# Low parts of weight blocks by a negation on GpSimd and an adding DMA, in a two-layer diffusion backbone

## The chip, the cores and the metric

The kernel runs on one core of one Trainium2 chip, in one launch. The metric is the device time of that launch in microseconds. Engines are named as in the profile: PE is TensorE (matmuls), DVE is VectorE, ACT is ScalarE, POOL is GpSimd, SP is SyncE, which issues nearly all DMAs here.

## The reference

Two layers of a backbone over 256 latent tokens and 256 context tokens, model width 1024, float32 throughout. Each layer is a half-step SwiGLU FFN, a mixing step and a second half-step FFN, each with adaLN shift, scale and gate computed from a condition vector.

```python
def ffn_sublayer(x, m, i, g, w_in, w_out):
    u = modulate(rms_norm(x, g), m, i)
    return x + 0.5 * m[:, 3 * i + 2][:, None] * swiglu(u, w_in, w_out)

# mixing, per layer
p = u @ w_in                    # q, k, v, Fourier input, gate logits
a = (rms_norm(attn_heads, subln_g) * (1 - lam_init)) @ w_attn_out
fr = fourier_mix(f) @ w_four_out
merged = sigmoid(ga + b_gate[0]) * a + sigmoid(gf + b_gate[1]) * fr
x = x + gate * (merged @ w_o)
```

Attention is differential (two softmax maps per head). The context stream is needed only until layer 1 has its keys and values: from there on, the merge, the output projection and the last FFN work on the latent tokens alone. A final RMSNorm gives the output.

## The kernel before

Activations stand transposed: features on the 128 partitions, tokens along the free dimension, 512 columns for both streams (latent and context) and 256 for the latent one alone. Every float32 product is made of three fast matmuls. A number is split into a high part, rounded to the matmul's format (`F32R`), and a low part, the rest; `mm3` (L370 to L375) accumulates high x high, high x low and low x high. `mm_wide` (L377 to L381) does the same for 256 columns with two matmuls, the first one over both parts of the activations at once.

The weights, 392 blocks of 128 x 1024 float32 (512 KB each, eight 128 x 128 tiles), pass through the class `Stream`. Its steps for a block:

- `load_to` (L176): SP issues the DMA of the raw block into a slot, `wraw`.
- `split_pieces` (L192, L193): ACT copies `wraw` to `whi`, which rounds it; then DVE or POOL computes `wlo = wraw - whi`.
- `next` hands out block b. It first issues loads up to b + `ahead[0]` and splits up to b + `ahead[1]`. `ahead` is (6, 2) while both streams are computed, (7, 4) in the last FFN and (7, 3) in the merge of layer 1.

The string `lo_on` says who subtracts: its letter at position i modulo its length stands for block i, "v" for DVE, "p" for POOL. All instructions run in the order in which the code issues them on each engine (`manual_schedule`); waits between engines follow from the tiles. `wraw`, `whi`, `wlo`, the activations `u` and `g` and more share one pool of 46 slots of 4 KB per partition, so a load also waits until the slot it takes over is free.

In an FFN the loop over j (L663 on) takes two blocks per step, one for `pa` and one for `pb`; ACT and DVE then make `silu(pa) * pb` (`silu`, `gv`) and split it into `g`. `project_out` multiplies `g` or the merged branches by the output weights (`po`). In layer 0, `tick` adds to every block two dot products on DVE (`junk`, L302) of condition weights (`mraw`, loaded by SP, 512 KB each) and every other time a small POOL instruction `mval` (L315, L317); these make the adaLN values. POOL also adds up squares for the norms (`acc`, L424).

The stages whose splits the change touches are the FFNs, the merge with its gates (`pg`, `pao`, `pfo`) and the output projection; the heads' projections, the values and the very first blocks keep DVE and POOL as before.

Of the kernel before, what the change touches and what calls it, by code (L numbers as in the profile page):

```python
# [11 lines left out]
F32 = mybir.dt.float32  # L12
F32R = mybir.dt.float32r
BF16 = mybir.dt.bfloat16
AF = mybir.ActivationFunctionType
ALU = mybir.AluOpType
# [21 lines left out]
LAT, CTX = 0, 1  # L38
# [33 lines left out]

BEGUN = 3

E_AHEAD, E_LO, E_K = 4, "vp", 2

SQ_PARTS = [7, 5]

# [80 lines left out]
    return rope.reshape(P, 4 * S), np.ascontiguousarray(dft.astype(np.float32))  # L159


class Stream:


# [15 lines left out]
    def split_pieces(self, n):  # L180

        nc = self.nc
        i = self.n_split
        self.n_split += 1
        raw = self.raw.pop(i)
        hi = self.pool.tile([P, 1024], F32R, tag="s", name="whi")
        lo = self.pool.tile([P, 1024], F32R, tag="s", name="wlo")
        self.hl[i] = (hi, lo)
        eng = nc.gpsimd if self.lo_on[i % len(self.lo_on)] == "p" else nc.vector
        for j in range(n):  # L190
            c = slice(j * (1024 // n), (j + 1) * (1024 // n))
            nc.scalar.activation(hi[:, c], raw[:, c], AF.Copy)  # L192
            eng.tensor_tensor(out=lo[:, c], in0=raw[:, c], in1=hi[:, c].bitcast(F32), op=ALU.subtract)  # L193
            yield
# [25 lines left out]
def tile_kernel(ctx: ExitStack, tc, d, out):  # L220
    nc = tc.nc
# [134 lines left out]
    st = Stream(nc, slot, blocks)  # L356
# [142 lines left out]
    def project_out(l, i, ss, k_of, n_k, after, next_set):  # L499

        nss = after[2] if after else [LAT]
        norm = Norm()
        u = [hilo(f"u{j}") for j in range(KC)] if after else None
        e = Unnormed(u, after) if after and len(ss) == 1 else None
        w = []

        def take(n):
            while len(w) < n:  # L510
                w.extend(st.tiles(8))
            got = w[:n]
            del w[:n]
            return got

        n_last = (1 if n_k > KC else 3) if len(ss) > 1 else 1
        c = cols(ss)
        wide = len(ss) == 1 and n_k == NF

        def product(ps, w, k, first, last):  # L520
            if wide:
                mm_wide(ps, w, k_of(k), c, first, last)
            else:
                mm3(ps[:, c], w, parts(k_of(k), c), first, last)

        begun = {}
        if n_k == KC:
            for m in range(BEGUN):
                begun[m] = bank("po"), take(n_k)
                for k in range(n_k - 1):  # L530
                    mm3(begun[m][0][:, c], begun[m][1][k], parts(k_of(k), c), k == 0, False)
        for m in range(KC - n_last):
            ps, tiles = begun.pop(m) if m in begun else (bank("po"), take(n_k))
            if m == 1:
                nc.scalar.preload_act_table_set(LN_EXP)
                if l == 0 and i == 0:
                    lambdas()
            if m:
                norm.add(m - 1, nss)
                if e:  # L540
                    e.chunk(m - 1)
            for k in range(n_k - 1 if m < BEGUN and n_k == KC else 0, n_k):
                product(ps, tiles[k], k, k == 0, k == n_k - 1)
            residual(m, ps, l, i, ss, wide)
        tiles = {m: take(n_k) for m in range(KC - n_last, KC)}
        norm.add(KC - n_last - 1, nss)
        if e:
            e.chunk(KC - 2)
            st.lo_on = "p"
            st.split_to(st.pos + E_AHEAD)  # L550
        later = None
        for s in ss:
            c = cols([s])
            steps = None
            for m in range(KC - n_last, KC):
                ps = bank("po")
                for k in range(n_k):
                    mm3(ps[:, c], tiles[m][k], parts(k_of(k), c), k == 0, k == n_k - 1)
                    if later and k == 7:
                        steps = later(False)  # L560
                        later = None
                        some(steps, STEPWISE[n_last == 1][0])
                residual(m, ps, l, i, [s])
                if e:
                    e.chunk(KC - 1)
                if s in nss and (m < KC - 1 or len(ss) > 1):
                    norm.add(m, [s])
                if steps and m < KC - 1:
                    some(steps, STEPWISE[n_last == 1][m - KC + n_last + 1])
            if not after:  # L570
                final_gain()
            if steps:
                some(steps, STEPWISE[n_last == 1][-1])
                st.split_to(st.pos + AHEAD)
                some(steps, KC)
            if s in nss:
                sq = norm.square(KC - 1, [s]) if len(ss) == 1 else None

                def later(last, s=s, sq=sq):
                    r = norm.total(s, sq)  # L580
                    if e:
                        e.r = r
                    if after:
                        yield from modulated(u, after[0], after[1], s, r)
                    else:
                        final(r)
                    if last and after:
                        nc.scalar.preload_act_table_set(next_set)

        def rest():  # L590
            some(later(True), KC + 1)

        if not after:
            return rest(), None
        return e or u, rest

    def ffn(l, f, ss, u, later, after):
        i = 2 * f
        g = {}
        e = None  # L600
        if isinstance(u, Unnormed):
            e, u = u, u.u
        st.ahead, st.lo_on, st.tick = (6, 2), "vvp", None
        if len(ss) == 1:
            st.ahead, st.lo_on = (7, E_AHEAD), E_LO
        if l == 0 and f == 1:
# [69 lines left out]
    def mixing(l, ss, u, later, after):  # L676
# [383 lines left out]
        nc.scalar.preload_act_table_set("silu_and_others")  # L1060
        merged = {}
        four = []
        st.ahead, st.lo_on = ((6, 2), "vvp") if CTX in ss else ((7, 3), "v")
        for m in range(KC):
            for n in range(2):
                if (m, n) in gates:
# [146 lines left out]
    def start(first, w, u):  # L1213

        n_q = 2 * first
        st.lo_on = "v"

        def weights_to(k):
            while len(w) < (k + 1) * n_q:
                b = st.pos  # L1220
                st.pos += 1
                st.load_to(b + 6)
                st.split_to(b)
                hi, lo = st.hl.pop(b)
                w.extend((hi[:, i * P:(i + 1) * P], lo[:, i * P:(i + 1) * P]) for i in range(8))

        sq = squares(LAT)
        nc.scalar.preload_act_table_set(LN_EXP)
        nc.gpsimd.tensor_scalar(out=bm1, in0=b_mod, scalar1=1.0, scalar2=1.0, op0=ALU.mult, op1=ALU.add)
        first_mod(0)  # L1230
        first_norm(LAT, sq)
        first_sum(0)
        first_u(0, [LAT])
        weights_to(0)
        ps = [bank("pf") for _ in range(n_q)]

        def products(k, ss, qs):
            c = cols(ss)
            for q in qs:
                mm3(ps[q][:, c], w[k * n_q + q], parts(u[k], c), k == 0 and ss[0] == LAT, k == KC - 1 and ss[-1] == CTX)  # L1240

        every = range(n_q)
        busy(ps[-1], 6)
        sq = squares(CTX)
        products(0, [LAT], every)
        first_mod(1)
        first_norm(CTX, sq, 4)
        first_sum(1)
        first_u(1, [LAT])
        weights_to(1)  # L1250
        first_u(0, [CTX])
        products(1, [LAT], every)
        first_mod(2)
        first_u(1, [CTX])
        products(0, [CTX], every)
        first_sum(2)
        first_u(2, both)
        weights_to(2)
        products(1, [CTX], every)
        first_mod(3)  # L1260
        for k in range(2, KC):
            products(k, both, every[:2])
            if k + 1 < KC:
                first_sum(k + 1)
                first_u(k + 1, both)
                weights_to(k + 1)
            if k == 5:
                nc.scalar.preload_act_table_set(SILU)
                for n in range(2):
                    nc.scalar.activation(cond[n], cond[n], AF.Silu)  # L1270
            if k == 6:
                st.lo_on = "vp"
                st.split_to(st.pos)
            if k == 7:
                st.split_to(st.pos + 1)
            products(k, both, every[2:])
            if k + 2 < KC:
                first_mod(k + 2)
        t = temp("lt")
        for n in range(2 * DEPTH):  # L1280
            o = 2 * n * HD
            nc.vector.scalar_tensor_tensor(
                out=t[:, :HD], in0=lamp[:, o:o + HD], scalar=1.0, in1=lamp[:, o + HD:o + 2 * HD], op0=ALU.mult, op1=ALU.mult,
                accum_out=lsum[:, n:n + 1],
            )
        st.lo_on = "vvp"
        return ps

    lsum = tiny.tile([P, 4], F32, tag="ls", name="lsum")
# [67 lines left out]
```

## Time and profile before

| | us |
|---|---|
| median of 2 runs (2012.07 and 2017.01) | 2014.54 |
| the profiled execution's own time | 2016.41 |
| its span, first to last instruction | 2014.5 |
| PE busy | 1992.3 |
| DVE / ACT / POOL busy | 1211.7 / 823.0 / 735.6 |

The clock that the throttle granted PE was 0.997 of full speed on average. Busy times of several engines overlap, so they don't add up to the span. In a group's row the figures after the first bar are its busy time in us and the mean of one instruction in ns, after the second bar the idle time of its engine just ahead of it and what ended most of it. Before the change no DMA is issued by POOL; 295 MB go through SP's queue.

### The profile page before, as it was taken

What the parts mean: (1) busy time and instruction counts of PE and PEld (TensorE: products, weight loads), DVE (VectorE), ACT (ScalarE), POOL (GpSimd) and SP (SyncE); (2) the same over time, 40 slices, a digit from 0 to 9 for tenths busy, and PEclk for the clock granted to TensorE, in tenths of its full rate; (3) what the DMA queues carried; (4) which work ended last, traced back from release to release, by engine and by line L of the source; (5) the groups of instructions that cost most, each with busy time, mean ns of one, the idle gap of its engine ahead of it and who ended that gap; (6) DMA issues with size and microseconds to landing.
All of it is one profiled execution on the core that took longest, in us unless ns stands there. A gap on an engine that the chain in (4) does not pass through costs nothing.

```text
span 2014.5 us, 26969 instructions
## 1 busy us (share of the span) xinstructions
PE 1992.3 (99%) x10388; PEld 1702.2 (84%) x10388; DVE 1211.7 (60%) x1832; ACT 823.0 (41%) x1335; POOL 735.6 (37%) x492
## 2 busy tenths in 40 slices
PE   8999999999999999999999999999999999999998
PEld 7888888888888888988888898888888889898887
DVE  5877786667777334677777252332324687776652
ACT  3432232256666323523223242222323565666661
POOL 0334455546553013243358410111222454224463
PEclk9999999999999999999999999999999999999999
DMA  9555565413222334455569332222421333555461
GB/s 378 204 169 176 167 210 210 165 58 110 92 85 93 105 105 137 157 172 173 178 212 353 104 131 82 91 74 84 139 91 53 126 128 119 192 172 193 158 203 59
DMA packets 86704, 297.58 MB, mean 148 GB/s; under 512 B 10032, under 2 KB 13232, under 8 KB 86576
## 3 DMA queue, kind: packets, MB, share of 16 engines
q1 hardware_dynamic: 86288, 295.34, 43.7%
q8 instruction: 81, 1.33, 0.3%
q10 hardware_dynamic: 288, 0.52, 0.1%
q14 instruction: 47, 0.39, 0.1%
HBM read 287.44 MB, written 1.05 MB: 143 GB/s over the span
## 4 chain that ended last, share of the span: by engine, by line
PE 93%; DVE 3%; ACT 2%; issue 1%; POOL 1%; DVEq 0%; POOLq 0%; ACTq 0%
PE po L375 7%; PE po L374 7%; PE po L373 7%; PE pa L373 5%; PE pb L375 5%; PE pa L375 5%; PE pb L373 5%; PE pa L374 5%; PE pb L374 5%; PE pg L373 2%; PE pg L375 2%; PE pg L374 2%; PE po L380 2%; PE pb L380 2%; PE pa L380 2%; PE pv L696 1%
## 5 line engine op out<-in xcount | busy, mean ns | idle before, releaser
L193 POOL TENSOR_TENSOR wlo<-wraw,whi 128x1024 fp32r<-128x1024 f32 x139 | 366.0, 2635 | 605.4 <-ACT whi L192 487.1
L192 ACT ACTIVATE whi<-wraw 128x1024 fp32r<-128x1024 f32 x392 | 395.5, 1049 | 74.8 <-PE po L374 34.1
L193 DVE TENSOR_TENSOR wlo<-wraw,whi 128x1024 fp32r<-128x1024 f32 x253 | 350.3, 1394 | 117.9 <-ACT whi L192 116.3
L302 DVE SCALAR_TENSOR_TENSOR junk<-mraw,cond 128x1024 bf16<-128x1024 f32 x224 | 303.1, 1395 | 1.1 <-DMA mraw<-in_w_mod 1.1
L373 PE MATMUL po<-g,whi 128*128 128x512 f32 (+1 forms) x616 | 223.8, 363 | 0.0
L375 PE MATMUL po<-g,wlo 128*128 128x512 f32 (+1 forms) x616 | 223.3, 362 | 0.0
L374 PE MATMUL po<-g,whi 128*128 128x512 f32 (+1 forms) x616 | 223.3, 362 | 0.0
L627 ACT ACTIVATE g<-gv 128x512 fp32r<-128x512 f32 (+1 forms) x92 | 51.7, 562 | 373.6 <-DVE gv L626 344.0
L317 POOL TENSOR_SCALAR mval<-macc,small 128x2 f32<-128x2 f32 (+1 forms) x88 | 122.3, 1394 | 216.2 <-DVE junk L302 216.2
L373 PE MATMUL pa<-u,whi 128*128 128x512 f32 x472 | 183.6, 389 | 0.0
L374 PE MATMUL pa<-u,whi 128*128 128x512 f32 x472 | 183.6, 389 | 0.0
L375 PE MATMUL pa<-u,wlo 128*128 128x512 f32 x472 | 183.6, 389 | 0.0
L373 PE MATMUL pb<-u,whi 128*128 128x512 f32 x472 | 183.6, 389 | 0.0
L374 PE MATMUL pb<-u,whi 128*128 128x512 f32 x472 | 183.6, 389 | 0.0
L375 PE MATMUL pb<-u,wlo 128*128 128x512 f32 x472 | 183.6, 389 | 0.0
L626 DVE TENSOR_TENSOR gv<-silu,pb 128x512 f32<-128x512 f32 x59 | 40.6, 688 | 182.3 <-PE pb L375 181.3
L462 DVE SCALAR_TENSOR_TENSOR x<-po,mval,x 128x256 f32<-128x256 f32 x73 | 32.6, 479 | 194.5 <-PE po L375 194.5
L374 PEld LDWEIGHTS po<-g,whi 128*128 128x128 f32 x616 | 116.3, 189 | 18.3
L373 PEld LDWEIGHTS po<-g,whi 128*128 128x128 f32 x616 | 116.2, 189 | 18.3
L375 PEld LDWEIGHTS po<-g,wlo 128*128 128x128 f32 x616 | 116.2, 189 | 17.9
L424 POOL TENSOR_TENSOR acc<-acc,sq 128x256 f32<-128x256 f32 (+1 forms) x46 | 53.2, 1156 | 191.5 <-ACT sq L413 191.5
L413 ACT ACTIVATE sq<-x 128x256 f32<-128x256 f32 (+1 forms) x48 | 24.7, 516 | 235.3 <-DVE x L462 202.8
(262 smaller groups left out, 4555.2 us busy)
## 6 DMA issues: line engine op xcount, KB each, us to landing
wraw<-in_ffn_in SPq DMA_DIRECT2D x176, 512.0 KB, 4.2
mraw<-in_w_mod SPq DMA_DIRECT2D x128, 512.0 KB, 3.7
wraw<-in_ffn_out SPq DMA_DIRECT2D x88, 512.0 KB, 4.4
wraw<-in_qk SPq DMA_DIRECT2D x32, 512.0 KB, 4.0
wraw<-in_g SPq DMA_DIRECT2D x32, 512.0 KB, 4.4
mfirst<-in_w_mod_first SPq DMA_DIRECT2D x16, 512.0 KB, 10.2
wraw<-in_v SPq DMA_DIRECT2D x16, 512.0 KB, 4.1
wraw<-in_attn SPq DMA_DIRECT2D x16, 512.0 KB, 4.0
```

What stands on the lines that cost most here:

```text
L192: nc.scalar.activation(hi[:, c], raw[:, c], AF.Copy)
L193: eng.tensor_tensor(out=lo[:, c], in0=raw[:, c], in1=hi[:, c].bitcast(F32), op=ALU.subtract)
L302: nc.vector.scalar_tensor_tensor(out=tmp.tile([P, D], BF16, tag="t", name="junk"), in0=mod_raw[n], scalar=1.0, in1=cond[s], op0=ALU.mult, ...
L317: eng.tensor_scalar(out=o, in0=v, scalar1=b_mod[:, b:b + 1], scalar2=0.5 if i % 3 == 2 else 1.0, op0=ALU.add, op1=ALU.mult)
L373: nc.tensor.matmul(ps, hi, uh, start=first, stop=False)
L374: nc.tensor.matmul(ps, hi, ul, start=False, stop=False)
L375: nc.tensor.matmul(ps, lo, uh, start=False, stop=last)
L380: nc.tensor.matmul(ps.rearrange("p (a b) -> p a b", a=2), hi, t[:, :, c], start=first, stop=False)
L424: nc.gpsimd.tensor_tensor(out=self.acc[:, c], in0=self.acc[:, c], in1=sq[:, c], op=ALU.add)
L462: nc.vector.scalar_tensor_tensor(out=x[:, m, c], in0=ps[:, c], scalar=mod(l, 3 * i + 2, m, s), in1=x[:, m, c], op0=ALU.mult, op1=ALU.add)
L626: nc.vector.tensor_tensor(out=v[:, c], in0=sl[:, c], in1=pb[:, c], op=ALU.mult)
L627: nc.scalar.activation(g[j][:, 0, c], v[:, c], AF.Copy)
```

## The change

For the blocks of the stages above, the letter is now "d". ACT copies the raw block to `whi` as before. POOL then writes `wlo = -whi` (one input instead of two), and a DMA issued by POOL adds the float32 raw block onto it, from slot to slot in the core's own memory (`accum_op=add`): `wlo = -whi + wraw`. 310 of the 392 splits take this way; of these DVE had 203 and POOL 107.

```diff
-E_AHEAD, E_LO, E_K = 4, "vp", 2
+E_AHEAD, E_LO, E_K = 4, "d", 2
...
+def split_by_dma(nc, hi, lo, raw):
+
+    nc.scalar.activation(hi, raw, AF.Copy)
+    nc.gpsimd.tensor_scalar(out=lo, in0=hi.bitcast(F32), scalar1=-1.0, scalar2=0.0, op0=ALU.mult, op1=ALU.add)
+    nc.gpsimd.dma_start(out=lo, in_=raw, accum_op=ALU.add)
...
-        eng = nc.gpsimd if self.lo_on[i % len(self.lo_on)] == "p" else nc.vector
+        on = self.lo_on[i % len(self.lo_on)]
+        if on == "d":
+            split_by_dma(nc, hi, lo, raw)
+            for j in range(n):
+                yield
+            return
+        eng = nc.gpsimd if on == "p" else nc.vector
...
-            st.lo_on = "p"                                                            # project_out
+            st.lo_on = E_LO
...
-        st.ahead, st.lo_on, st.tick = (6, 2), "vvp", None                             # ffn
+        st.ahead, st.lo_on, st.tick = (6, 2), "d", None
...
-        st.ahead, st.lo_on = ((6, 2), "vvp") if CTX in ss else ((7, 3), "v")          # mixing
+        st.ahead, st.lo_on = ((6, 2), "d") if CTX in ss else ((7, 3), "d")
...
-        st.lo_on = "vvp"                                                              # start
+        st.lo_on = "d"
```

Line numbers after the new function are 7 higher in the changed kernel, and 13 higher from the split on. Two places show what moved. The first is POOL's queue in the first FFN of layer 0, where `mval` stands between the splits; before:

```order
L193 TENSOR_TENSOR wlo_922<-wraw_753,whi_921 128x1024
L317 TENSOR_SCALAR mval_83<-macc_82,small_73 128x2 x3
L193 TENSOR_TENSOR wlo_1042<-wraw_873,whi_1041 128x1024
L317 TENSOR_SCALAR mval_83<-macc_82,small_73 128x2 x3
L193 TENSOR_TENSOR wlo_1171<-wraw_1002,whi_1170 128x1024
```

and in the changed kernel:

```order
L165 TENSOR_SCALAR wlo_1013<-whi_1012 128x1024
L166 DMA wlo_1013<-wraw_840 128x1024
L330 TENSOR_SCALAR mval_83<-macc_82,small_73 128x2
L165 TENSOR_SCALAR wlo_1051<-whi_1050 128x1024
L166 DMA wlo_1051<-wraw_878 128x1024
L330 TENSOR_SCALAR mval_83<-macc_82,small_73 128x2
```

POOL had one subtraction per three blocks; now every block has a negation and a DMA there, and the DMA waits for the negation ahead of it and for the load of its raw block. The second place is the last FFN of layer 1, the latent stream alone, on DVE (`g12`, `g13` are the gated products); before:

```order
L193 TENSOR_TENSOR wlo_16235<-wraw_16140,whi_16234 128x1024
L386 TENSOR_TENSOR silu_16277<-pa_16230,silu_16277 128x256
L386 TENSOR_TENSOR gv_16278<-pb_16231,gv_16278 128x256
L622 TENSOR_TENSOR gv_16278<-silu_16277,gv_16278 128x256
L631 TENSOR_TENSOR g12_16276<-gv_16278,g12_16276 128x256
L193 TENSOR_TENSOR wlo_16292<-wraw_16197,whi_16291 128x1024
```

and now:

```order
L399 TENSOR_TENSOR silu_16551<-pa_16502,silu_16551 128x256
L399 TENSOR_TENSOR gv_16552<-pb_16503,gv_16552 128x256
L635 TENSOR_TENSOR gv_16552<-silu_16551,gv_16552 128x256
L644 TENSOR_TENSOR g12_16550<-gv_16552,g12_16550 128x256
L399 TENSOR_TENSOR silu_16610<-pa_16561,silu_16610 128x256
```

DVE's subtraction, one of every two blocks, is gone from between the gated products. In the last output projection POOL's queue now reads like this (`acc` sums the squares for the final norm):

```order
L437 TENSOR_TENSOR acc_17183<-acc_17183,sq_17253 128x256
L165 TENSOR_SCALAR wlo_17306<-whi_17305 128x1024
L166 DMA wlo_17306<-wraw_17232 128x1024
L165 TENSOR_SCALAR wlo_17313<-whi_17312 128x1024
L166 DMA wlo_17313<-wraw_17239 128x1024
L437 TENSOR_TENSOR acc_17183<-acc_17183,sq_17317 128x256
```

where one subtraction stood between two sums before:

```order
L424 TENSOR_TENSOR acc_16885<-acc_16885,sq_16952 128x256
L193 TENSOR_TENSOR wlo_17005<-wraw_16934,whi_17004 128x1024
L424 TENSOR_TENSOR acc_16885<-acc_16885,sq_17014 128x256
L193 TENSOR_TENSOR wlo_17067<-wraw_16946,whi_17066 128x1024
L193 TENSOR_TENSOR wlo_17079<-wraw_17008,whi_17078 128x1024
```

ACT's and SP's instructions keep their order.

## Prediction

> **What bounds the kernel now.** I read the head of the page first, then its chain of waits, then a table of windows.
>
> ```profile
> span 2014.5 us, 26969 instructions
> PE 1992.3 (99%) x10388; PEld 1702.2 (84%) x10388; DVE 1211.7 (60%) x1832; ACT 823.0 (41%) x1335; POOL 735.6 (37%) x492
> PE 93%; DVE 3%; ACT 2%; issue 1%; POOL 1%; DVEq 0%; POOLq 0%; ACTq 0%
> L193 POOL TENSOR_TENSOR wlo<-wraw,whi 128x1024 fp32r<-128x1024 f32 x139 | 366.0, 2635 | 605.4 <-ACT whi L192 487.1
> L192 ACT ACTIVATE whi<-wraw 128x1024 fp32r<-128x1024 f32 x392 | 395.5, 1049 | 74.8 <-PE po L374 34.1
> L193 DVE TENSOR_TENSOR wlo<-wraw,whi 128x1024 fp32r<-128x1024 f32 x253 | 350.3, 1394 | 117.9 <-ACT whi L192 116.3
> ```
>
> TensorE is busy 1992.3 of 2014.5 us and is 93% of the chain. It is idle for only 22.2 us (2014.5 - 1992.3) in the whole program, so no edit that leaves the matmuls alone can gain more than 1.1%. The work that the change takes away, the rows named L193, is done by engines that are 60% and 37% busy. The question is therefore whether what replaces it is ready as early as before. For that the program is cut into its stages; the columns are the stretch, its length, each engine's busy time, the granted clock, the DMA share and the rate.
>
> ```profile
> core 0: us, PE busy (x) PEld busy (x) DVE busy (x) ACT busy (x) POOL busy (x), PEclk, DMA share, GB/s
> 66.00:395.00 329.00, 329.00 (x1513) 275.04 (x1512) 248.64 (x354) 93.86 (x119) 153.09 (x95) 1.00 0.53 183
> 650.00:823.00 173.00, 173.00 (x871) 147.86 (x870) 71.09 (x101) 61.49 (x89) 32.82 (x19) 1.00 0.39 127
> 823.00:1178.00 355.00, 355.00 (x1693) 299.44 (x1693) 237.34 (x338) 106.73 (x141) 158.27 (x97) 1.00 0.55 188
> 1178.00:1552.00 374.00, 373.69 (x1802) 315.86 (x1802) 129.92 (x155) 113.79 (x156) 70.49 (x35) 1.00 0.29 95
> 1735.00:2005.00 270.00, 268.48 (x1777) 245.04 (x1776) 162.44 (x241) 149.90 (x253) 106.43 (x72) 1.00 0.51 167
> ```
>
> These five stretches are where the changed splits lie: first FFN, merge and output projection, second FFN of layer 0 (66 to 395, 650 to 823, 823 to 1178), first FFN of layer 1 (1178 to 1552), then its merge, output projection and last FFN (1735 to 2005). TensorE is idle for 0.31 + 1.52 us in them: **there is nothing to win here**, at most 2 us. The last stretch is the tight one. It computes 256 columns instead of 512, so it eats weight blocks almost twice as fast: 92 blocks (18 merge, 8 projection, 66 FFN) in 270 us, 2.9 us each.
>
> **What a transfer may cost.** The second half of layer 0 holds a stretch in which the DMA engines had all the work they could take. The first two rows are the busy tenths and the rate in 40 slices of 1060 to 1178 us, then a landing time from there; the last row is from 1178 to 1420 us, a calm stretch.
>
> ```profile
> DMA  9999999994489979925232750560040000000089
> GB/s 419 404 410 410 411 405 408 412 410 194 90 274 330 361 250 393 379 74 165 35 149 75 283 172 6 178 175 3 22 161 0 0 0 0 0 0 0 6 310 385
> mraw<-in_w_mod SPq DMA_DIRECT2D x18, 512.0 KB, 7.3
> wraw<-in_ffn_in SPq DMA_DIRECT2D x30, 512.0 KB, 3.6
> ```
>
> Nine slices stand at about 410 GB/s. I take that as the capacity: a pass over one block (512 KB, 524,288 bytes) is 1.28 us of all sixteen engines. A load lands 3.6 us after its issue when calm, so 2.3 us of it is fixed; in the crowd it takes 7.3.
>
> **The change part by part.** 310 of 392 splits change: 57 + 29 + 66 + 66 + 92 in the five stretches. DVE loses 203 subtractions (203 x 1.394 = 283 us), GpSimd 107 (107 x 2.635 = 282 us). Both were off the path, so I book **0 us** of gain. ACT's copy stays as it is.
>
> GpSimd gains 310 negations and 310 DMA issues. Its one-input instructions by shape, a tiny instruction of it, and one of SyncE's DMA issues:
>
> ```profile
> L826 POOL TENSOR_SCALAR p<-p,rs 128x512 f32<-128x512 f32 x32 | 22.4, 699 | 26.9 <-DVE rs L825 25.5
> L826 POOL TENSOR_SCALAR p<-p,rs 128x256 f32<-128x256 f32 x16 | 7.5, 483 | 1.1 <-DVE rs L825 0.4
> L317 POOL TENSOR_SCALAR mval<-macc,small 128x2 f32<-128x2 f32 x64 | 93.3, 1458 | 191.3 <-DVE junk L302 191.3
> 1081.95 0.33 SPq L176 DMA_DIRECT2D wraw<-in_ffn_out  x1
> ```
>
> 256 more elements cost 699 - 483 = 216 ns, so 1024 cost 699 + 432 = 1.13 us. How long GpSimd is held by issuing a DMA no row shows, since this kernel issues none there. The lower end is SyncE's 0.33 us, the upper one a whole two-input pass, 2.6 us; I take 1.0, nearer to SyncE's issue because it is the same act, but with a tiny GpSimd instruction at 1.46 in mind. That is 2.1 us per block, below the 2.9 us of the tight stretch. The DMA waits on GpSimd for the negation just ahead of it, and the next block's negation, mval and the norm's sums queue behind; in layer 0 mval in turn waits there for DVE's dot products. None is late if the issue is near 1 us.
>
> The transfer itself has no row either. It reads wraw, reads wlo and writes wlo, all in SBUF, where a load reads once and writes once. Lower end: as a load, one pass, 1.28 us. Upper end: three passes, 3.84 us. I take two, 2.56 us, because two tensors are read for one written, and the load's row already contains its write. One sentence from the Trainium skill, Collectives: The Full Stack (The bandwidth ceiling): a reducing DMA runs at about half a copy's rate, since both sources are read through one ring; by it the price would be an estimated 2 x 1.28 = 2.56 us, and no run here shows it yet.
>
> **Throughput, stage by stage** (rate x length / 410, plus accumulations x 2.56):
> - 66 to 395: 183 x 329 = 60 MB, 147 us; 57 x 2.56 = 146; together 293 of 329 us.
> - 650 to 823: 54 + 74 = 128 of 173 us.
> - 823 to 1178: 163 + 169 = 332 of 355 us.
> - 1178 to 1552: 87 + 169 = 256 of 374 us.
> - 1735 to 2005: 167 x 270 = 45 MB, 110 us; 92 x 2.56 = 235; together 345 of 270 us: **75 us too much.** The DMA engines become the bound of that stretch, and TensorE waits for wlo.
>
> **Lateness in the wide stages.** There the capacity suffices, but the path from ACT's copy to the first matmul on wlo grows. Rows from an FFN pair of blocks in 1178 to 1552:
>
> ```profile
> 1302.07 1.99 ACT L192 ACTIVATE whi<-wraw 128x1024 fp32r<-128x1024 f32 x2
> 1300.54 0.39 PE L373 MATMUL pa<-u,whi 128*128 128x512 f32 x1
> 1311.42 0.39 PE L373 MATMUL pa<-u,whi 128*128 128x512 f32 x1
> 1311.87 0.39 PE L375 MATMUL pa<-u,wlo 128*128 128x512 f32 x1
> ```
>
> A pair of blocks takes 10.88 us. The two copies that start at 1302.07 are for the next pair, and its first low part is read at 1311.87. The first copy is done at 1303.06, the negation at 1304.2, which leaves 7.7 us. Issue 1.0 + fixed 2.3 + 2.56 = 5.9 us: 1.8 us to spare. In 1060 to 1178 the crowd adds 7.3 - 3.6 = 3.7 us, so each of some 11 pairs (118 / 10.88) is 1.9 us late, 21 us; for the other two layer-0 FFN stretches at 89 to 94% use I add 4. Lateness: **25 us**. Late landings also hold the raw slot longer, and SyncE's loads queue for slots; six blocks ahead in the wide stages hide that, seven ahead at 2.9 us may not, which is inside the 75.
>
> Sum: 75 + 25 = 100 us on the profiled execution's own 2016.4 us (2014.5 us of span and 1.9 around it), which is 0.1% from the median of 2014.5: **2116 us**, 5% slower.
>
> **A rule weighed.** What decides is that loads and accumulations share engines: SyncE alone filled them to 410 GB/s above. The Trainium skill, DMA: Bandwidth & Descriptors (Issuing engines are not separate DMA queues), says that DMAs of SyncE, ScalarE and GpSimd end on the same sixteen engines and interleave. It speaks against this change; with it the sum stands, without it 235 us would fit into 270 and the 75 us would vanish. The rows of one issuing queue cannot show which.
>
> **The rivals.**
> - **Not slower (chance 0.25).** One place and price decide it: in 1735 to 2005 the accumulation must cost under (270 - 110) / 92 = 1.74 us. At the one-pass 1.28 the stretch needs 228 of 270 us, nothing waits, and wide pairs have 3 us spare: 2016 to 2030 us, say 2022. For it: SBUF on both sides, no HBM. Against: two reads.
> - **Three passes (0.13).** 3.84 us each: 110 + 353 = 463 against 270, +193; 66 to 395, 147 + 219, +37; 823 to 1178, 163 + 253, +61; the others still fit. +291: 2307 us.
> - **GpSimd becomes the bound (0.12).** If an issue costs 2.6 us, a block costs 3.73, 92 x 3.73 = 343 us plus about 15 of sums: +88 in the last stretch, in place of the DMA engines' 75; with 10 us of lateness, 2114 us. For it: the tiny mval at 1.46 us. The same time, told apart by who is busy.
> - **Faster (0.03).** DVE's lighter load shortens the stage changes; at most 22 us, so 1995 us, within 2%.
>
> **How the numbers follow.** The forecast has 0.47, its own range is 2060 to 2170 (half to one and a half of the sum). 80%: from 2020, which cuts off the fastest part of the not-slower case and the faster one, to 2310, the three passes. A measurement of this kernel tells about 2% from no change. Slower by over 2% (above 2055): 0.47 + 0.13 + 0.12 less 0.01 = 0.71; within 2%: 0.27; faster: 0.02.
>
> **What would show it.** A GpSimd queue with 163 MB (310 blocks) in the DMA section; in 1735 to 2005 DMA share at 0.9 and TensorE idle by about 75 us, waiting for a DMA on wlo; 1178 to 1552 unchanged; negations near 1.13 us. Wrong if that last stretch stays at 270 us (accumulation under 1.74 us), if TensorE waits in 1178 to 1552 (landing over 7.7 us), or if GpSimd is busy without a gap in the last stretch.

## The result, and the profile after

| | us |
|---|---|
| median after (2 runs, 2194.18 and 2199.91) | 2197.05 |
| forecast (range) | 2116 (2020 to 2310) |
| ratio to before | 1.0906, 95% interval 1.0822 to 1.099 |
| the profiled execution's own time, its span | 2194.18, 2192.4 |

The kernel is 9% slower. First the head of the page after: the span, the engines, the busy tenths of the DMA engines, the two large queues (packets, MB, share of sixteen engines), the chain of waits, the two new groups of GpSimd, and the landing time of the new DMA.

```profile
span 2192.4 us, 27988 instructions
PE 2040.8 (93%) x10388; PEld 1721.3 (79%) x10388; DVE 950.8 (43%) x1629; ACT 826.6 (38%) x1335; POOL 1024.5 (47%) x1005
DMA  9799999722333877899999877779843337999998
q0 software_dynamic: 44640, 162.55, 39.4%
q1 hardware_dynamic: 86288, 295.34, 38.0%
issue 33%; PE 33%; POOL 19%; DMA 12%; DVE 2%; ACT 1%; POOLq 0%; SPq 0%; DVEq 0%; ACTq 0%
L165 POOL TENSOR_SCALAR wlo<-whi 128x1024 fp32r<-128x1024 f32 x310 | 391.0, 1261 | 508.1 <-ACT whi L164 473.6
L166 POOL DMA_DIRECT2D wlo<-wraw x310 | 277.6, 896 | 175.4 <-POOL wlo L165 102.9
wlo<-wraw POOLq DMA_DIRECT2D x310, 512.0 KB, 7.7
```

TensorE's part of the chain fell from 93% to 33%. The accumulations (q0) took 39.4% of the sixteen engines' span: 0.394 x 2192.4 / 310 = 2.79 us of all sixteen each, as much in sum as all the loads (q1), though they move 55% as many bytes. A load of the same size took 0.380 x 2192.4 / 563.3 = 1.48 us (295.34 MB are 563.3 blocks). The same stretches as before the change, at their new places:

```profile
67.00:417.00 350.00, 333.78 (x1509) 274.19 (x1509) 197.89 (x312) 94.06 (x119) 197.42 (x194) 1.00 0.95 262
694.00:854.00 160.00, 152.32 (x723) 127.97 (x722) 32.87 (x57) 48.47 (x66) 59.54 (x61) 0.98 0.77 190
854.00:1258.00 404.00, 375.08 (x1756) 311.05 (x1755) 190.94 (x305) 110.26 (x147) 216.20 (x209) 0.98 0.93 258
1258.00:1626.00 368.00, 363.71 (x1746) 307.12 (x1745) 52.90 (x96) 107.80 (x145) 138.96 (x140) 1.00 0.78 186
1837.00:2184.00 347.00, 281.47 (x1696) 245.63 (x1695) 86.81 (x171) 147.23 (x241) 185.98 (x214) 0.96 1.01 254
```

In the last stretch the DMA share is 1.01 and GpSimd is busy for 186 of 347 us. The share adds up the time of packets, and it can pass 1: before the change, loads alone stood at 1.03 from 1060 to 1086 us, where they moved 410 GB/s. TensorE is idle for 66 us of the stretch; the three largest of its waits there, by line (us in total, times, longest):

```profile
PE pa L394 <- DMA wlo<-wraw: 15.3, 13, 4.9
PE pb L394 <- DMA wlo<-wraw: 12.4, 14, 1.7
PE po L394 <- DMA wlo<-wraw: 11.6, 14, 1.9
```

Cut at TensorE's first matmul of each stage (by tile: `pa` for FFN in, `po` for FFN out and projection, `pao` for the merge, `pf` for an FFN's first pairs, `pv` for the values; the last stretch ends with the last matmul), the 178 us of longer span (2192.4 - 2014.5) lie as follows; the runs of the next section stand beside them, in us over before:

| stage (us before) | after | one more ahead | quarter mod loads | deeper everywhere | plain copy | all causes gone |
|---|---|---|---|---|---|---|
| FFN 0 of layer 0, in and out (327.7) | +22 | +22 | +10 | +18 | +1 | +3 |
| heads and values, both layers (477.5) | +10 | 0 | +11 | 0 | +5 | 0 |
| merge and projection, layer 0 (148.3) | +12 | 0 | +12 | 0 | +5 | 0 |
| FFN 1 of layer 0, first pairs (23.5) | +6 | +2 | +6 | +2 | +5 | +1 |
| FFN 1 of layer 0, in and out (338.6) | +36 | +19 | +7 | +18 | +6 | +2 |
| FFN 0 of layer 1 (362.9) | +6 | 0 | +6 | 0 | +4 | 0 |
| last stretch (260.2) | +87 | +86 | +88 | +83 | +27 | +1 |

Outside the last stretch the change costs 91 us, where the forecast had 25; in it 87, where the forecast had 75.

### The profile page after: what moved, and what is told of

It is laid out like the page before. It is cut to its first block, busy times and chain, and to the rows that moved or that the text cites. A ratio compares the mean times of both kernels' runs of the same rounds, so it can differ in the third digit from the quotient of the medians.

```text
span 2192.4 us, 27988 instructions
## 1 busy us (share of the span) xinstructions
PE 2040.8 (93%) x10388; PEld 1721.3 (79%) x10388; DVE 950.8 (43%) x1629; ACT 826.6 (38%) x1335; POOL 1024.5 (47%) x1005
## 3 DMA queue, kind: packets, MB, share of 16 engines
q0 software_dynamic: 44640, 162.55, 39.4%
q1 hardware_dynamic: 86288, 295.34, 38.0%
HBM read 287.44 MB, written 1.05 MB: 132 GB/s over the span
## 4 chain that ended last, share of the span: by engine, by line
issue 33%; PE 33%; POOL 19%; DMA 12%; DVE 2%; ACT 1%; POOLq 0%; SPq 0%; DVEq 0%; ACTq 0%
POOL wlo L165 12%; DMA wlo<-wraw 9%; POOL wlo L166 4%; PE po L388 3%; PE po L387 3%; PE po L386 3%; DMA mraw<-in_w_mod 1%; PE pg L388 1%; PE pg L386 1%; PE pg L387 1%; PE pv L710 1%; PE pk L388 1%; PE pv L708 1%; PE pv L709 1%; PE pk L387 1%
## 5 line engine op out<-in xcount | busy, mean ns | idle before, releaser
L165 POOL TENSOR_SCALAR wlo<-whi 128x1024 fp32r<-128x1024 f32 x310 | 391.0, 1261 | 508.1 <-ACT whi L164 473.6
L164 ACT ACTIVATE whi<-wraw 128x1024 fp32r<-128x1024 f32 x310 | 313.2, 1047 | 157.2 <-DMA wlo<-wraw 37.0
L166 POOL DMA_DIRECT2D wlo<-wraw x310 | 277.6, 896 | 175.4 <-POOL wlo L165 102.9
L315 DVE SCALAR_TENSOR_TENSOR junk<-mraw,cond 128x1024 bf16<-128x1024 f32 x224 | 300.7, 1385 | 95.9 <-DMA mraw<-in_w_mod 95.1
L388 PE MATMUL po<-g,wlo 128*128 128x512 f32 (+1 forms) x616 | 225.8, 367 | 14.1 <-DMA wlo<-wraw 14.0
L206 POOL TENSOR_TENSOR wlo<-wraw,whi 128x1024 fp32r<-128x1024 f32 x32 | 85.2, 2663 | 127.7 <-ACT whi L205 85.7
L388 PEld LDWEIGHTS pa<-u,wlo 128*128 128x128 f32 x472 | 89.4, 189 | 45.4 <-DMA wlo<-wraw 26.8
L330 POOL TENSOR_SCALAR mval<-macc,small 128x2 f32<-128x2 f32 (+1 forms) x88 | 98.7, 1121 | 50.2 <-DVE junk L315 43.7
```

Source lines behind the costliest of these rows:

```text
L164: nc.scalar.activation(hi, raw, AF.Copy)
L165: nc.gpsimd.tensor_scalar(out=lo, in0=hi.bitcast(F32), scalar1=-1.0, scalar2=0.0, op0=ALU.mult, op1=ALU.add)
L166: nc.gpsimd.dma_start(out=lo, in_=raw, accum_op=ALU.add)
L315: nc.vector.scalar_tensor_tensor(out=tmp.tile([P, D], BF16, tag="t", name="junk"), in0=mod_raw[n], scalar=1.0, in1=cond[s], op0=ALU.mult, ...
L330: eng.tensor_scalar(out=o, in0=v, scalar1=b_mod[:, b:b + 1], scalar2=0.5 if i % 3 == 2 else 1.0, op0=ALU.add, op1=ALU.mult)
L388: nc.tensor.matmul(ps, lo, uh, start=False, stop=last)
```

## The experiments

**Where the time lies.** Both runs keep the letter "d" for a part of the blocks and give the others their old letter (`old`):

```diff
         on = self.lo_on[i % len(self.lo_on)]
+        if on == "d" and i < len(self.blocks) - 92:     # last_stretch_only; >= in all_but_last
+            on = self.old[i % len(self.old)]
```

> The negation and the accumulating DMA only in the last stretch (merge, output projection and last FFN of layer 1, 88 blocks); everywhere else the subtractions of before. Full DMA engines (loads and accumulations share the sixteen): the last stretch takes as long as with the whole change, 347 us against 260 before, so 2014.5 + 87 = 2101 us, 2095 to 2107. If the stretch were long because of something that the earlier stages leave behind (late loads, full slots), it would shrink: under 2070.

Measured: 2103.86 us, ratio 1.0446 (1.043 to 1.0462), with a last stretch of 346 us.

> The counterpart: the change everywhere but in the last stretch, whose 88 splits are subtractions again. If the two parts are independent, 2197 - 87 = 2110 us, 2100 to 2115, with the last stretch at 260 us. Full DMA engines: the 91 us stay in layer 0, in stages that also load mraw; the first FFN of layer 1, which loads none, stays within 6 us of before.

Measured: 2109.85 us, ratio 1.0481 (1.0455 to 1.0507), with a last stretch of 257 us; layer 1's first FFN was 7 us longer, where at most 6 had been expected. The parts are nearly independent: 89.9 + 95.9 = 186 us over the runs of before beside them (2013.91), against 182.5 for the whole change.

**What a transfer costs.** Two runs leave GpSimd's 310 negations and 310 issues and change what the DMA moves:

```diff
-    nc.gpsimd.dma_start(out=lo, in_=raw, accum_op=ALU.add)
+    nc.gpsimd.dma_start(out=lo.bitcast(F32), in_=raw)                              # plain_copy
+    nc.gpsimd.dma_start(out=lo[:, :512], in_=raw[:, :512], accum_op=ALU.add)       # half_columns
```

> The DMA copies the raw block onto the low part instead of adding it: one source read instead of two, the same 310 negations and 310 issues on GpSimd, the same bytes written. Full DMA engines with an accumulation of 2.79 us of sixteen engines and a load of 1.48: the copy takes about 1.4, the last stretch needs 110 + 88 x 1.4 = 233 of 260 us and is back to 260 to 270; the layer-0 stages lose most of their delay; 2030 to 2050 us in all. GpSimd as the bound (negation 1.26 + issue 0.89 + waits): nothing changes, 2190 to 2200. A fixed delay of a GpSimd DMA, whatever it moves: nothing changes either.

> The accumulating DMA covers 512 of the 1024 columns of each block (the other half of the low part stays the negated high part): two source reads, half the bytes, as many instructions and issues as the change. Full DMA engines: 2.79 / 2 = 1.4 us per block, so as the plain copy, 2030 to 2050 us, the last stretch at 260 to 270. GpSimd as the bound or a fixed delay: 2190 to 2200. If the rows of 2 KB cost as much as those of 4 KB (a price per descriptor): 2190 to 2200 as well, with the DMA share of the GpSimd queue still near 39%.

Measured: 2068.49 us for the copy, ratio 1.0267 (1.0249 to 1.0286), and 2085.74 for half the columns, 1.0369 (1.0345 to 1.0393). GpSimd's queue share, issue and landing, of the copy's page and then of that with half the columns:

```profile
q0 software_dynamic: 44640, 162.55, 20.6%
L166 POOL DMA_DIRECT2D wlo<-wraw x310 | 180.7, 583 | 125.4 <-POOL wlo L165 120.1
wlo<-wraw POOLq DMA_DIRECT2D x310, 512.0 KB, 4.5
```

```profile
q0 software_dynamic: 44640, 81.28, 22.9%
L166 POOL DMA_DIRECT2D wlo<-wraw x310 | 277.1, 894 | 128.6 <-POOL wlo L165 118.2
wlo<-wraw POOLq DMA_DIRECT2D x310, 256.0 KB, 4.9
```

The copy of 512 KB costs 0.206 x 2067.7 / 310 = 1.37 us of sixteen engines, the addition of the same bytes 2.79 (2.04 times as much), the addition of half of them 0.229 x 2082.9 / 310 = 1.54. So the price goes nearly with the bytes, and one per descriptor alone is excluded (as many packets, half the bytes, 55% of the time). That the second read is what doubles it was not shown: the addition also writes `lo` as `F32R`, where the copy writes it as plain float32, and no run takes these apart. With as many GpSimd instructions 111 to 129 us of the 182 went, so neither GpSimd nor a fixed delay alone holds the kernel; with half the columns GpSimd was even held as long for each issue. But both runs missed their 2030 to 2050: the last stretch needs 233 of 260 us by my sum and took 288 and 292. The engines' share there stood below one, in the copy's run at 0.83:

```profile
1772.00:2060.00 288.00, 267.84 (x1697) 242.87 (x1696) 83.15 (x171) 146.21 (x242) 156.11 (x214) 0.96 0.83 306
```

Of the copy's run 54.6 us over before remain, 27 of them in this stretch, so something beside full engines costs time. For the next four runs I followed each block in the trace of the changed kernel (k-th copy, k-th negation, k-th DMA; means over a stage's blocks, in us):

| stage | copy's end to negation | negation | issue to landing | copy's start to landing |
|---|---|---|---|---|
| FFN in, layer 1's first FFN | 0.65 | 1.21 | 5.8 | 9.1 |
| FFN in, layer 0's second FFN | 2.14 | 1.39 | 7.3 | 12.3 |
| FFN out, layer 0's second FFN | 8.14 | 1.23 | 8.8 | 19.7 |
| merge, layer 1 | 0.56 | 1.19 | 7.8 | 11.1 |
| FFN in, last FFN | 0.91 | 1.20 | 10.0 | 14.1 |

Two suspects for layer 0 were GpSimd's queue, where `mval` waits for DVE's dot products with the next negation behind it, and the mraw loads on the same engines.

```diff
-        mod_affine(nc.gpsimd, n, slice(0, ns))
+        mod_affine(nc.vector, n, slice(0, ns))                                      # mval_on_dve
...
-            nc.sync.dma_start(t, d["w_mod"][l, q])
+            nc.sync.dma_start(t[:, :256], d["w_mod"][l, q][:, :256])                # quarter_mod_loads
...
-        st.ahead, st.lo_on, st.tick = (6, 2), "d", None
+        st.ahead, st.lo_on, st.tick = (7, 3), "d", None                             # one_more_ahead, and
...
-        st.ahead, st.lo_on = ((6, 2), "d") if CTX in ss else ((7, 3), "d")
+        st.ahead, st.lo_on = ((7, 3), "d") if CTX in ss else ((7, 3), "d")
```

> The changed kernel with the modulation values (mval) computed on DVE, right behind the dot products they need, instead of on GpSimd. In the changed kernel's trace the negation starts 2.1 us after ACT's copy has ended in the wide FFN-in stages of layer 0 and 8 to 10 us after it in their FFN-out stages, against 0.65 us in the first FFN of layer 1, where no mval is in the queue. GpSimd's queue as the cause of the layer-0 delay: these gaps fall to about 0.7 us, and the FFN stages of layer 0, 64 us over before, come down to 10 to 25 over: 2140 to 2160 us. Crowded DMA engines as the cause: the gaps fall as well, but the landings stay at 7 to 9 us and the stages long: 2180 to 2197.

Measured: 2195.46 us, ratio 1.0903 (1.0861 to 1.0946). **The queue theory fell.** The gap did shrink (from 2.14 to 0.99 us in the second FFN's in-stage, from 8.14 to 2.04 in its out-stage), but in the in-stage the landings grew by about as much, as these rows show (changed kernel, then this run; medians):

```profile
wlo<-wraw POOLq DMA_DIRECT2D x39, 512.0 KB, 7.1
```

```profile
wlo<-wraw POOLq DMA_DIRECT2D x40, 512.0 KB, 8.2
```

There a DMA that was issued sooner landed hardly sooner (12.0 us from the copy's start instead of 12.3). In the out-stage the path did fall, from 19.7 to 14.1 us, and this FFN was 26 us over before instead of 36; but the first FFN of layer 0 was 28 over instead of 22, and the whole stayed as long.

> The changed kernel with mraw loads of 256 instead of 1024 columns; each dot product goes over that quarter four times, so that DVE works as long as before. It leaves out three quarters of the modulation weights. Crowded DMA engines as the cause of the layer-0 delay: 48 MB and about 130 us of the engines' time go, landings fall from 7.4 to the 5.8 us of the first FFN of layer 1, and the FFN stages of layer 0 come down from 64 us over to under 20 over: 2140 to 2155 us. GpSimd's queue (mval waiting for the dot products) as the cause: those gaps stay, 2180 to 2197.

Measured: 2157.32 us, ratio 1.0713 (1.0686 to 1.074), just above the 2140 to 2155. The landing of the accumulations in that in-stage fell to 5.9 us, and the two FFNs of layer 0 to +10 and +7 us:

```profile
wlo<-wraw POOLq DMA_DIRECT2D x40, 512.0 KB, 5.9
```

The crowd is real, but the merge, the heads and the stage changes stay as late as before.

> The changed kernel with one block more of lookahead in the stages with 512 columns: loads 7 and splits 3 ahead instead of 6 and 2, so a split has 5.4 us longer before its low part is read. A path that is too long for its lookahead (path 12.3 us from the start of ACT's copy to landing, about 11 available) as the cause of the layer-0 delay: it vanishes, 2100 to 2130 us, the last stretch as before at 347. Full DMA engines in layer 0 (share 0.90 to 0.96): nothing is won by starting earlier, 2185 to 2200. Too few slots: the loads start later, slower than 2200.

Measured: 2144.45 us, ratio 1.0645 (1.0629 to 1.0661), in between. The two FFNs of layer 0 kept +22 and +19 us: their in-stages are within 4 us of before, and the delay now lies in the out-stages (19 and 18 us; 4 and 16 in the changed kernel). The windows over each of them fit full engines: the DMA share, next to last, stands at 0.97 and 0.98.

```profile
66.00:416.00 350.00, 335.14 (x1508) 278.90 (x1507) 207.23 (x314) 93.16 (x120) 202.41 (x197) 0.98 0.97 265
863.00:1220.00 357.00, 344.84 (x1558) 285.41 (x1557) 177.72 (x274) 95.85 (x121) 196.08 (x199) 0.99 0.98 276
```

Merge, projection, heads and layer 1's first FFN, where the engines have time left, are back to their old length. So layer 0's delay has two causes: a path too long for its lookahead, and, as the run with both causes relieved below confirms, full engines.

> The negation and the accumulating DMA only in the last stretch, and there for every second block (44 of 88); the others are subtractions as before. Full DMA engines: loads 110 us and 44 x 2.79 = 123 us make 233 of 260 us, so nothing is full and the time is 2015 to 2030 us. A path too long for the lookahead of seven loads and three or four splits: every such block is late as before and half the delay or more stays, 2050 to 2100.

```diff
+        if on == "d" and (i < len(self.blocks) - 92 or i % 2):
+            on = self.old[i % len(self.old)]
```

Measured: 2074.45 us, ratio 1.0298 (1.0282 to 1.0313): **my reading of the last stretch was half the story.** With engines that are not full, 58 of the 87 us stayed:

```profile
1747.00:2065.00 318.00, 277.11 (x1695) 248.82 (x1693) 131.13 (x183) 143.32 (x242) 180.06 (x158) 0.94 0.77 204
```

In its projection and last FFN the other half of the blocks are subtractions on GpSimd (2.67 us each), which a cleaner run would not have. The next three runs give the last stretch more lookahead too, 9 loads and 6 splits.

```diff
-E_AHEAD, E_LO, E_K = 4, "d", 2
+E_AHEAD, E_LO, E_K = 6, "d", 2
...
-            st.ahead, st.lo_on = (7, E_AHEAD), E_LO
+            st.ahead, st.lo_on = (9, E_AHEAD), E_LO
...
-        st.ahead, st.lo_on = ((6, 2), "d") if CTX in ss else ((7, 3), "d")
+        st.ahead, st.lo_on = ((7, 3), "d") if CTX in ss else ((9, 6), "d")          # (6, 2) in every_second_deeper
```

> The whole change with more lookahead in every stage that it touches: loads 7 and splits 3 ahead where 512 columns are computed (as in the run with one more ahead), loads 9 and splits 6 ahead in the last stretch (instead of 7 and 3 or 4). Full DMA engines in the last stretch: its 45 MB of loads and 46 MB of accumulations moved at 270 GB/s with a share of 1.05, so at least 335 us stay of the 347, and 2130 to 2145 us in all. A path too long for the lookahead (13 us from ACT's copy to landing, about 11 available): the stretch comes down to 260 to 280 us, 2055 to 2080 us.

Measured: 2139.09 us, ratio 1.062 (1.0604 to 1.0635). The last stretch took 344 us against 347: the splits start earlier (18.6 us from ACT's copy to landing in the merge instead of 11.1) and only 4 us are won. The engines are full:

```profile
1786.00:2130.00 344.00, 287.06 (x1696) 248.61 (x1694) 95.94 (x171) 147.36 (x242) 186.46 (x214) 0.95 1.01 256
```

> The accumulating DMA for every second block of the last stretch alone, the other blocks' subtractions all on DVE, loads 9 and splits 6 ahead. Without more lookahead that stretch took 318 us, with a DMA share of only 0.69 to 0.81 in its long parts. The lookahead as the cause of those 58 us: with full engines far off (233 of 260 us needed) they vanish, 2014 to 2025 us. If they stay (2060 to 2075), something else holds every accumulation back, such as GpSimd's in-order queue.

Measured: 2025.29 us, ratio 1.0058 (1.0036 to 1.0079). The same lookahead that won 4 us with 88 accumulations won 47 with 44 (318 to 271 us). In the FFN the move of the other subtractions to DVE has a part in it that was not separated. In the merge, where the other blocks are DVE subtractions in both runs, only the lookahead differs, and its delay fell from 21 to 7 us, most of the 10 that are left. The whole stretch:

```profile
1745.00:2016.00 271.00, 261.27 (x1695) 237.36 (x1693) 128.20 (x215) 143.62 (x242) 104.44 (x126) 0.99 0.90 240
```

> The deeper lookahead of the other run, and the engines relieved: mraw loads of 256 columns (the dot products go over that quarter four times) and, in the last stretch alone, a plain copy instead of the addition. It leaves out three quarters of the modulation weights and the low parts' sum in the last stretch; the 310 negations, the 310 GpSimd DMAs and the accumulations outside the last stretch are all there. If lookahead and full DMA engines are the only causes, no stage is more than a few us over before: 2015 to 2030 us. What is left above that is a third cause.

```diff
-            nc.sync.dma_start(t, d["w_mod"][l, q])
+            nc.sync.dma_start(t[:, :256], d["w_mod"][l, q][:, :256])
...
+    if add:                                                                  # i < len(self.blocks) - 92
+        nc.gpsimd.dma_start(out=lo, in_=raw, accum_op=ALU.add)
+    else:
+        nc.gpsimd.dma_start(out=lo.bitcast(F32), in_=raw)
```

Measured: 2024.64 us, ratio 1.0055 (1.0034 to 1.0076), inside its 2015 to 2030: with both causes relieved, 171 of the 178 us of span are gone while all 310 negations and GpSimd DMAs are still there. Against the run with more lookahead alone, smaller mraw loads take layer 0's FFNs from +18 and +18 to +3 and +2 us, and copies in place of additions take the last stretch from +83 to +1. The last stretch, at the copy's price and with the deeper lookahead:

```profile
1752.00:2013.00 261.00, 257.32 (x1694) 234.79 (x1692) 89.45 (x171) 144.38 (x241) 155.19 (x214) 1.00 0.90 338
```

GpSimd has 155 us of work in 261 (186 with additions in the changed kernel), so it isn't a third cause. The share of 0.90 over the stretch, with no delay left, also says that a high share alone doesn't prove full engines; that the delay goes when they are relieved does.

> The negation and the accumulating DMA only in the stages where, with loads 7 and splits 3 ahead, neither cause was left: merge and output projection of layer 0 and the first FFN of layer 1 (90 blocks, with that lookahead); everywhere else the subtractions and the lookahead of before. If lookahead and full DMA engines are all that the change costs, these 90 accumulations are free: 2012 to 2018 us, no stage more than 1 us longer than before. It cannot be faster by more than a few us, TensorE being idle for 22 us in all before. If the change costs something that is not tied to a stage (90 x 0.6 us, the 182 us shared out evenly over 310 blocks, is 53 us), 2030 to 2070 us.

```diff
+        if on == "d" and not (101 <= i < 130 or 196 <= i < 262):
+            on = self.old[i % len(self.old)]
...
+        if l == 1 and f == 0:
+            st.ahead = (7, 3)
```

Measured: 2019.3 us, ratio 1.0028 (1.0015 to 1.004), just above what was expected. Every stage stands within 1 us of before or under it, but for the first pairs of layer 1's first FFN: 29.1 instead of 24.3 us, with one wait in them, by the list of TensorE's waits (us in total, times, longest):

```profile
PE pf L390 <- DMA wlo<-wraw: 4.0, 1, 4.0
```

TensorE waits once, for 4.0 us, on the low part. There the stage before still runs two splits ahead, which probably starts the first accumulations of the new stage late: with one more ahead in all stages it was 24.3. The other accumulations are hidden. No version here beats the kernel before, whose TensorE is idle for 22 us in all.

## Why the prediction was right or wrong

The direction and the main mechanism, full DMA engines in the last stretch, came as forecast; the size did not, 182 us where 100 were forecast. 2197 us lies in the wide range only because that takes in the rival of three passes; the forecast's own range, 2060 to 2170, was missed.

**What bounds the kernel, and the gain of 0: right.** DVE went from 1211.7 to 950.8 us of work, and nothing came of it.

**The price of an accumulation: right in ratio, 9% low in size.** I took two passes, 2.56 us, and 2.79 were measured, 2.04 times a plain copy between the same memories. The Trainium skill, Collectives: The Full Stack (The bandwidth ceiling), has about half a copy's rate for the reducing DMAs of a collective: the trace agrees for an addition within SBUF. The page's reason, two source reads, no run here separates from the rest of the addition. The sum's 1.28 us for a load was a rate that only the best slices reach; in the mix it took 1.48. With these prices the second FFN of layer 0 (355 us at 188 GB/s before the change, 66.7 MB or 127 blocks, and 66 accumulations) needs 127 x 1.48 + 66 x 2.79 = 372 of its 355 us, where I had 332: it is full, and the run with one more ahead kept 19 us there.

**GpSimd's prices: right.** Issue 0.90 us (taken 1.0), negation 1.26 us (taken 1.13). It is no bound, as said.

**The last stretch, 75 us: near in size (87), incomplete in cause.** Two errors offset each other in part: of the 92 blocks counted, 88 went by the DMA (310 less the 222 of the run without this stretch), and each cost 2.79 us. 110 + 88 x 2.79 = 356 of 270 us would have been 86 too much. "The DMA engines become the bound of that stretch" holds when the lookahead is long enough (344 us). But at the lookahead that the kernel has, 58 us stay at half the accumulations, where the engines are not full; with GpSimd's subtractions in between, that is the path's share as near as the runs tell it. Either cause would have been enough for most of the delay. I had left that aside with "which is inside the 75".

**Lateness, 25 us: the step that failed; it was 91.** Three faults. I let the crowd reach 118 us of layer 0 and booked 4 us for its other FFN stretches; in fact the accumulations make the crowd themselves, wherever mraw is loaded too (share 0.95 and 0.93 over both layer-0 windows): the FFNs cost 58 instead of 25. I worked the spare time out for an FFN in full flow alone, 1.8 us, and it did hold in the one calm stage (217.6 us before and after for its in-stage); but its first pairs took 5 us more, so "1178 to 1552 unchanged" did not hold. The places where the lookahead has to be built up (merge, projection, heads, the first pairs of an FFN) were not in the sum at all: 34 us. And in the second FFN of layer 0 the path held more GpSimd queueing than in layer 1's first FFN, by 1.5 us in the in-stage and 6 us in the out-stage, which I had called never late, though the run with `mval` on DVE shows that its removal alone buys nothing in all.

**A term that I did not have: the clock.** Around waits of TensorE the granted clock falls to a half for 3.4 or 6.8 us: in the changed kernel at each of the twelve waits of 3.6 us or longer, and at five of the eight of 1.9 to 3.3 us. By the trace's record of that clock the changed kernel has 19 intervals at half clock with 80 us in all, against 3 with 14 us before; 66 us more at half speed are worth at most 33 us. It is part of TensorE's longer busy time, 2040.8 against 1992.3 us for the same 10388 matmuls: of the last stretch's 87 us some 64 are idle time and 23 are matmuls that take longer.

**The rivals.** Not slower fell at its own point, 1.74 us (2.79 measured); three passes fell by the same number; GpSimd as the bound fell to the run with half the columns, where its work in the last stretch was the same 186 us and the stretch 55 us shorter, and to those 186 us being of 347. The rule that issuing engines share the sixteen DMA engines (the Trainium skill, DMA: Bandwidth & Descriptors, Issuing engines are not separate DMA queues) agrees with the trace: the last stretch stood at a share of 1.01 with both queues together, and GpSimd's DMAs landed 1.2 us sooner when only SyncE's mraw loads were made smaller (7.1 to 5.9).

## What to carry to other kernels

In this kernel, moving work from an engine that is off the path to the DMA engines was free only where two things were left: engine time (here 2.8 us of all sixteen per 512 KB added in SBUF, twice a copy) and lookahead (here at least 7.1 us from the copy's start to the landing, where copy and subtraction took 1.05 + 1.39 = 2.4 on DVE and 1.05 + 2.64 = 3.7 on GpSimd). Test them apart: half the transfers relieve the engines but not the path, more lookahead relieves the path but not the engines, and a stretch that gives back little to one of them alone, and all to both, has both causes. Sum a new latency at every stage change too, not in full flow only, and add the clock that longer waits take away.

## What the runs showed of the hardware

**The clock falls with single waits.** A piece of the last output projection, the wait (in brackets) and matmuls behind it, then two at full clock, and windows over both:

```profile
1907.75 0.58 PE L388 MATMUL po<-mg,wlo 128*128 128x256 f32 x1 [4.02 <-DMA wlo<-wraw]
1908.13 0.41 PE L386 MATMUL po<-mg,whi 128*128 128x256 f32 x1
1908.34 0.41 PE L387 MATMUL po<-mg,whi 128*128 128x256 f32 x1
...
1913.44 0.28 PE L386 MATMUL po<-mg,whi 128*128 128x256 f32 x1
1913.56 0.28 PE L387 MATMUL po<-mg,whi 128*128 128x256 f32 x1
```

```profile
1906.00:1912.80 6.80, 5.05 (x23) 5.05 (x24) 0.00 (x0) 3.05 (x3) 5.73 (x28) 0.50 1.05 310
1913.00:1916.00 3.00, 2.27 (x20) 2.06 (x18) 0.00 (x0) 0.00 (x0) 2.59 (x3) 1.00 1.02 291
```

The matmuls start every 0.21 us at a clock of 0.50 and every 0.12 us at 1.00, so a wait of 4.0 us cost some 2 us more behind it (an estimate: 5 us of matmuls at 0.21 instead of 0.12).

**The issue's price depends on the kind, not on the bytes.** GpSimd was held for 0.58 us by a copy, for 0.89 to 0.90 us by an addition, with rows of 4 KB or of 2 KB, and in the median an issue began 0.41 us after the negation that it waits for. A negation took 1.04 us alone; the 100 that started within 1 us of the start of an accumulating DMA's issue took 1.38 in the median, in the run with copies 1.06. Another 40, all beside one of DVE's dot products in layer 0's FFNs, took 1.7 to 2.0 us, and 44 did so with copies. Why the addition slows a negation was not tried.
